# S5 parameters laid out by the host with the walked index contiguous, and the within-chunk products formed for four column groups at a time

## The chip, the cores and the metric

The kernel runs on one core of a Trainium2 chip. The metric is device time in microseconds for one execution, from inputs in device memory to the output in device memory. Rearranging inputs on the host (transposing or copying arrays before the launch) is not part of that time.

The engines named below are TensorE (PE in the profile; its weight loads are PEld), VectorE (DVE), ScalarE (ACT), GpSimd (POOL) and SyncE (SP). SyncE issues nearly all DMAs of this kernel, in one queue and in program order.

## The reference

The program is a two-layer residual trunk over 256 tokens of 2048 channels in float32. Layer 0 mixes tokens by stick-breaking attention and gated linear attention, layer 1 by a block-diagonal state-space model (S5); each layer then has a SwiGLU feed-forward part. The part that matters here is S5. 128 groups of 16 channels have 64 complex states each:

```python
lb_re, lb_im = mag * jnp.cos(ang), mag * jnp.sin(ang)            # lambda, per group and state
bb_re = cr[..., None] * b_re - ci[..., None] * b_im              # B scaled; b: (group, p, h)
bu_re = jnp.einsum('blgh,gph->blgp', u, bb_re)
_, _, s_re, s_im = lax.associative_scan(combine, (a_re, a_im, bu_re, bu_im), axis=1)
y = (jnp.einsum('ghp,blgp->blgh', c_re, s_re)                    # c: (group, h, p)
     - jnp.einsum('ghp,blgp->blgh', c_im, s_im) + d_skip * u)
```

Here h is one of 16 channels of a group and p one of its 64 states. The kernel does not scan token by token: it takes 32 chunks of 8 tokens. For that it prepares, from the parameters alone, three sets of matrices per group: `win` (lambda^(7-j) B: from the tokens of a chunk into the state), `ed` (C lambda^m: from the state to the tokens) and `td` (the real part of C lambda^(j'-j) B, with D on its diagonal: from token to token inside a chunk).

## The kernel before, in words

**The linear layers.** All large products multiply the 256 tokens by streamed weights. A chunk of weights is 4 k-tiles by 512 columns, 1 MB, brought by one DMA on SP's queue (`wraw`, line 100, three buffers). Each chunk is split in two units of 2 k-tiles: ScalarE writes the high part (`whi`), VectorE the low part (`wlo`), five buffers each, and a unit is split three units before it is used. TensorE then runs 12 matmuls of 512 columns per unit (lines 190 to 192, high by high, high by low, low by high, for two token blocks). TensorE executes in program order.

**Background work.** After each unit the program calls `pump`. It advances a list of generators, each up to its next `yield`, as long as an estimate of VectorE and ScalarE time stays within a budget. `s5_prep` is such a generator. It has nothing to do with the layer being computed (the feed-forward part of layer 0) and only has to be through before layer 1 begins. One `yield` is thus one unit of the linear layer further on, 12 large matmuls. The instructions between two yields stand in each engine's queue at that place.

**What s5_prep does, in order.** It forms lambda and its powers (`lam`, 9 powers side by side, so one power of successive states lies 36 bytes apart). It scales B by a factor per state and the norm gain. ScalarE spreads B into `bb` and a DMA writes it to the array `bb_d` in device memory. Then 32 steps multiply C by powers of lambda: four multiplies, one subtraction and one combined operation of 128 x 288 elements on VectorE per step, into `ed` and `tt`, and a DMA to `e_d` (lines 1142 to 1157).

Then come the products within a chunk: 16 iterations k of two halves. For a half, four DMAs (`fetch`, line 1170) bring pieces of `e_d` and `bb_d` into one of two buffers in the tile `et`; TensorE multiplies them (line 1213) into two of the four 32-row column groups of an accumulator; ScalarE copies 64 rows of it to `kp`, which also lies in the tile `et`, in one of two slots. After both halves VectorE adds D. After every second k, eight DMAs write `kp` to `t_d` (line 1222). A half's pieces are fetched one half ahead (`nxt`). One k takes seven yields.

The generator `win` runs beside the products: 28 steps of four multiplies and two sums of 128 x 256 elements, and four copies by lambda to the power zero in two parts, each followed by a DMA to `win_d` (line 1194).

When the products, `win` and the input product of the feed-forward part are done, the loads of the first `win` matrices from device memory into the tiles `ring` are issued (line 1240); the remaining loads for S5 (`w`, `t`, the second filling of `ring`, `eb`: lines 1240, 1244, 1249) follow when layer 1 begins.

Of the kernel before, what the change touches and what calls it, by code (L numbers as in the profile page):

```python
"""One core: residual trunk (stick-breaking + GLA mixer, S5 mixer, SwiGLU) in Tile.

Every weight product runs as three float32r passes on exactly split operands:
w = wh + wl, x = xh + xl (each part 12 significant bits), xh.wh + xh.wl + xl.wh.
"""
# [46 lines left out]
class Eng:  # L52
    """An engine's builders; adds up an estimate of the time of what they emit."""
# [23 lines left out]
class Stream:  # L77
    """Weights: 4 k-tiles x 512 columns per DMA, split by 2 k-tiles, ahead of their use."""
# [45 lines left out]
    def fill_extra(self):  # L124
        """one unit more, into a buffer that another part of the program has left"""
        if self.extra and len(self.split) // 2 < len(self.loaded):
            self.convert(self.extra.pop(0))
            return 1
        return 0

    def reload(self):
        """the buffers of chunks that have been split are loaded anew, up to chunk `limit`, and lent from there on"""
        end = len(self.plan) if self.limit is None else self.limit
        while True:
            room = len(self.split) // 2 + self.raw_bufs
            if len(self.loaded) < min(end, room):
                self.load()
            elif self.loans and len(self.loaded) == end and end + self.lent < room:
                self.loans.pop(0)()
                self.lent += 1  # L140
            else:
                break

    def next(self, ahead):
        """the next unit; `ahead` units from it on are split when it returns"""
        self.fill(self.used + ahead)
        got, self.split[self.used] = self.split[self.used], None
        self.used += 1
        return got


class Kern:
# [5 lines left out]
    # ---- background work: generators advanced between the units of a linear layer.  # L158
    # They yield where another engine has to take over, or True where none has to.
# [34 lines left out]
    # ---- linear layer: out[tok, n] for 512-column blocks  # L194
    def linear(self, blocks, acts, evac, opening=None, mid=None, hooks=None, spare=None):
        """blocks: ids; acts: (hi, lo) per k-tile, each an AP [128, 256].
        opening(mm): emits the first units of the first block, returns how many.
        mid: token-block-major order over the last four units, mid() emitted within them;
        the second token block's evacuation is then left in self.tail.
        hooks: {unit of the first block: callable emitted ahead of it (unit + 0.5: after it)}  # L200
        spare(): buffers for units split ahead of the last block's end"""
# [50 lines left out]
    def pairwise(self, blocks, acts, evac, hooks):  # L252
        """two blocks side by side, chunk by chunk; hooks: {unit: callable emitted ahead of it}"""
# [24 lines left out]
    # ---- small pieces  # L278
    def rstds(self, sums, width=D, between=None):
        """1 / sqrt(sum(ss) / width + eps) of several [128, 4] partial sums of squares, step by step side by side"""  # L280
# [21 lines left out]
    def split_to(self, hi, lo, src, scale=None):  # L302
        """hi + lo = src * scale (scale: None or [128, 1]); src may be in PSUM"""
# [15 lines left out]
    def turn(self, tb, k4, gcol):  # L319
        """four k-tiles of h (token-major) -> acts, feature-major, times the norm gain, split"""  # L320
# [21 lines left out]
    def post(self, layer, which, final=False, hold=()):  # L342
        """the evacuation of a sub-layer's output: y -> h += rms_norm(y) * gain.
        returns evac(nb, tb, ps) and the part that closes a token block"""
# [45 lines left out]
    # ---- plan of the weight stream  # L390
# [32 lines left out]
    # ---- SwiGLU  # L423
    def ffn(self, layer, final, mid, enter):
        """enter(): closes the pools of the mixer, when the first units have been emitted"""
# [140 lines left out]
    # ---- layer 0: stick-breaking attention and GLA  # L566
# [89 lines left out]
    def feat(self, src, dst):  # L656
        """[128 tok, 2, 512] -> [128, 4, 256] feature-major"""
# [9 lines left out]
    def softplus_neg_abs(self, dst, src):  # L667
        """dst = log(1 + exp(-|src|))"""
        nc = self.nc
        nc.scalar.activation(dst, src, AF.Abs)  # L670
        nc.scalar.activation(dst, dst, AF.Exp, scale=-1.0)
        nc.scalar.activation(dst, dst, AF.Ln, bias=1.0)

    def gla_gate(self, n0, tb, ps, rs):
        """sr = silu(r) * gain, r = ps * rs"""
# [12 lines left out]
    def gla(self, rs):  # L688
# [3 lines left out]
        # low-rank gate  # L692
# [61 lines left out]
        # scores, transposed: S[s, head, t] (even heads, then odd ones) for the token-tile pairs (0,0), (0,1), (1,1)  # L754
# [23 lines left out]
        for li, b in enumerate((64, 32, 16, 8, 4, 2, 1)):  # L778
            yield from self.need(2 * b + 1)
            mix = self.got.pop(2 * b + 1)  # L780
            # only the later halves of the blocks of 2 b tokens take part as t; even and odd heads at once
# [16 lines left out]
        # outputs  # L798
# [43 lines left out]
    def gla_levels(self):  # L842
        """k exp(cum_mid - cum_s) in the first halves, q exp(cum_t - cum_mid) in the second ones, per block size"""
# [40 lines left out]
    def sb_group(self, g):  # L884
        """four stick-breaking heads"""
# [55 lines left out]
    # ---- layer 1: S5, 32 chunks of 8 tokens. Token t = 8 c + j; group 8 k + 2 q + e holds the  # L941
    # channels 128 k + 32 q + 16 e + h; its state p is at partition (e, p), column 4 k + q.
    def s5_prep(self):
        """chunk matrices of the state space, from its parameters (partition = group (e, 4 k + q)), to DRAM:
        win[(h, j), (ri, p)] = lam^(7-j) B, ed[p, (m, h')] = C lam^m, td[(h, j), (j', h')] = Re C lam^(j'-j) B (+ D)"""
# [50 lines left out]
        # sine and cosine of th  # L996
# [50 lines left out]
        # (lam - 1) / lambda  # L1047
# [16 lines left out]
        # lam^8 at (e, p), column 4 k + q  # L1064
# [32 lines left out]
        # B, times the norm gain  # L1097
        B = st("B").rearrange("g (r p h) -> g r p h", r=2, p=64)
# [4 lines left out]
        for p0 in range(0, 64, 16):  # L1103
            ps = slice(p0, p0 + 16)
            n = pw([128, 2, 16, 16], "bt")
            crb, cib = (c[:, ps].unsqueeze(2).to_broadcast([128, 16, 16]) for c in (cr, ci))
            gb = g16.unsqueeze(1).to_broadcast([128, 16, 16])
            V.tensor_mul(n[:, 0], cib, B[:, 1, ps])
            V.tensor_mul(n[:, 1], cib, B[:, 0, ps])
            V.tensor_mul(B[:, 0, ps], crb, B[:, 0, ps])  # L1110
            yield True
            V.tensor_mul(B[:, 1, ps], crb, B[:, 1, ps])
            V.tensor_sub(B[:, 0, ps], B[:, 0, ps], n[:, 0])
            V.tensor_add(B[:, 1, ps], B[:, 1, ps], n[:, 1])
            yield True
            V.tensor_mul(B[:, 0, ps], B[:, 0, ps], gb)
            V.tensor_mul(B[:, 1, ps], B[:, 1, ps], gb)
# [9 lines left out]
        for p0 in range(0, 64, 8):  # L1127
            flush()
            o = pw([128, 2, 8, 2, 16], "bb")
            for ri in range(2):  # L1130
                for e in range(2):
                    nc.scalar.activation(o[:, ri, :, e, :], B[:, ri, p0:p0 + 8], AF.Identity, scale=self.sel[:, e:e + 1])
            late.append(lambda o=o, p0=p0: dma(bb_g[:, :, p0:p0 + 8], o.rearrange("g r p e h -> g r p (e h)")))
            yield
        # C
        flush()
        C = st("C").rearrange("g (r h p) -> g r h p", r=2, h=16)
# [4 lines left out]
        for p0 in range(0, 64, 2):  # L1142
# [3 lines left out]
            c = [C[:, ri, :, p0:p0 + 2].rearrange("g h p -> g p h").unsqueeze(2).to_broadcast([128, 2, 9, 16]) for ri in range(2)]  # L1146
# [13 lines left out]
        # the products within a chunk  # L1160
# [12 lines left out]
        def win():  # L1173
            late = []
            for h0 in range(0, 16, 4):
                b = [B[:, ri, :, h0:h0 + 4].rearrange("g p h -> g h p") for ri in range(2)]
# [24 lines left out]
        nxt = fetch(0)  # L1201
        for k in range(16):
            for half in range(2):
                et, bt = nxt
                if 2 * k + half < 31:
                    nxt = fetch(2 * k + half + 1)
                yield
                yield
                p = self.pbig([128, 128])
                for ri in range(2):  # L1210
                    for q in range(2):
                        r = 64 * half + 32 * q
                        nc.tensor.matmul(p[r:r + 32, :], lhsT=bt[:, q, ri, :], rhs=et[:, q, ri, 0:128], start=(ri == 0), stop=(ri == 1))  # L1213
                yield
                pr = slice(64 * half, 64 * half + 64)
                nc.scalar.copy(kp[pr, k % 2, 112:240], p[pr])
# [17 lines left out]
    def s5_load(self, what, u, t):  # L1234
        """matrices of the groups of the channel tiles 2 u and 2 u + 1 ("t1", "e": of the channel tile u; "e" with zero between even and odd groups)"""
# [16 lines left out]
    def layer1(self):  # L1252
# [3 lines left out]
        def normed(tb, nb, r, eng):  # L1256
            """normalized h, without the gain, over the sub-layer's output"""
# [41 lines left out]
        def scan(hf):  # L1299
            """by pairs of chunks: within them, along the even chunks, from those to the odd ones;  # L1300
            yields where an operation waits for the one before it, four times in a step"""
# [143 lines left out]
        def out(G, n=0):  # L1445
            """channel tiles 4 G to 4 G + 3"""
# [81 lines left out]
def host_layout(inputs):  # L1528
    """the inputs as they are; the parameters of S5 with the even groups ahead of the odd ones"""
    arrays = {n: np.ascontiguousarray(inputs[n]) for n in INPUTS}  # L1530
    for n in INPUTS:
        if n.startswith("s5_") and n != "s5_d":
            a = arrays[n][0]
            arrays[n] = np.ascontiguousarray(a.reshape((64, 2) + a.shape[1:]).swapaxes(0, 1).reshape((1,) + a.shape))
# [16 lines left out]
```

## Time and profile before

| what | value |
|---|---|
| median of 3 runs | 2232.69 us (2229.08 to 2235.0) |
| span of the profiled execution | 2230.8 us (its time outside the span is not listed) |
| TensorE busy | 2175.5 us (98%) |
| VectorE busy | 1376.8 us (62%) |
| ScalarE busy | 985.1 us (44%) |
| DMA traffic | 456.36 MB, mean 205 GB/s |
| products within a chunk (line 1213) | 832.1 to 1176.9 us of the span, 256 matmuls |

In the profile, PE, PEld, DVE, ACT, POOL and SP are the engines, and "L1213" is line 1213 of the kernel. Most VectorE and ScalarE operations are recorded through one helper, line 65, so they are told apart by the tiles they write and read: `wlo<-wraw,whi` is the low part of a weight unit. A group row gives total busy time and the mean of one in nanoseconds, and behind the bar the idle time just before, with what ended it. In a timeline row the first number is the start in us from the span's beginning, the second the length of the merged run. TensorE's matmuls overlap: a large one is listed with 0.39 us though they start 0.23 us apart.

### The profile page before, as it was taken

What the parts mean: (1) busy time and instruction counts of PE and PEld (TensorE: products, weight loads), DVE (VectorE), ACT (ScalarE), POOL (GpSimd) and SP (SyncE); (2) the same over time, 40 slices, a digit from 0 to 9 for tenths busy, and PEclk for the clock granted to TensorE, in tenths of its full rate; (3) what the DMA queues carried; (4) which work ended last, traced back from release to release, by engine and by line L of the source; (5) the groups of instructions that cost most, each with busy time, mean ns of one, the idle gap of its engine ahead of it and who ended that gap; (6) DMA issues with size and microseconds to landing.
All of it is one profiled execution on the core that took longest, in us unless ns stands there. A gap on an engine that the chain in (4) does not pass through costs nothing.

```text
span 2230.8 us, 26592 instructions
## 1 busy us (share of the span) xinstructions
PE 2175.5 (98%) x10448; PEld 1751.4 (79%) x10448; DVE 1376.8 (62%) x1917; ACT 985.1 (44%) x1242; POOL 16.0 (1%) x19
## 2 busy tenths in 40 slices
PE   8999999999999999999998699999999999999998
PEld 6888888788888887777776578878888888888886
DVE  4676645658779997895456765475444444444545
ACT  5544545454544444334344434464444434433433
POOL 0000000000000000000000100000000000000000
PEclk9999999999999999999999999999999999999999
DMA  7454454554677678998779976546555545555543
GB/s 227 169 179 157 164 170 152 188 209 170 223 241 250 226 249 241 276 281 263 225 229 271 274 223 201 176 171 214 181 189 171 206 171 195 181 190 188 188 171 133
DMA packets 318653, 456.36 MB, mean 205 GB/s; under 512 B 31136, under 2 KB 127664, under 8 KB 318016
## 3 DMA queue, kind: packets, MB, share of 16 engines
q1 hardware_dynamic: 317808, 449.95, 62.3%
q0 software_dynamic: 720, 4.72, 0.6%
q8 instruction: 82, 1.34, 0.2%
q14 instruction: 43, 0.35, 0.0%
HBM read 424.21 MB, written 30.41 MB: 204 GB/s over the span
## 4 chain that ended last, share of the span: by engine, by line
PE 91%; DVE 3%; DMA 2%; ACT 1%; issue 1%; SPq 1%; POOL 0%; DVEq 0%; ACTq 0%; POOLq 0%
PE lin L190 28%; PE lin L192 28%; PE lin L191 28%; PE big L465 1%; DMA eb<-e_d 1%; DVE wlo L65 1%; PE big L1213 1%; PE big L192 0%; PE big L792 0%; PE big L191 0%; PE big L190 0%; DVE h L65 0%; DVE xl L65 0%; ACT xh L65 0%; DMA ring<-e_d 0%
## 5 line engine op out<-in xcount | busy, mean ns | idle before, releaser
L65 DVE TENSOR_TENSOR wlo<-wraw,whi 128x1024 fp32r<-128x1024 f32 x713 | 860.3, 1223 | 562.1 <-ACT whi L65 561.6
L65 ACT CAST whi<-wraw 128x1024 fp32r<-128x1024 f32 x713 | 731.3, 1049 | 650.3 <-PE lin L192 575.1
L190 PE MATMUL lin<-whi,xh 128*128 128x512 f32 x2016 | 803.1, 398 | 3.5 <-ACT xh L65 3.5
L191 PE MATMUL lin<-wlo,xh 128*128 128x512 f32 x2016 | 796.9, 395 | 2.3 <-DVE wlo L65 2.1
L192 PE MATMUL lin<-whi,xl 128*128 128x512 f32 x2016 | 796.6, 395 | 0.9 <-DVE xl L65 0.9
L190 PEld LDWEIGHTS lin<-whi,xh 128*128 128x128 f32 x2016 | 380.2, 189 | 95.2 <-issue 5.0
L191 PEld LDWEIGHTS lin<-wlo,xh 128*128 128x128 f32 x2016 | 380.2, 189 | 91.2 <-DVE wlo L65 5.7
L192 PEld LDWEIGHTS lin<-whi,xl 128*128 128x128 f32 x2016 | 380.0, 188 | 90.9 <-DVE xl L65 2.5
L190 PE MATMUL lin<-whi,ah 128*128 128x512 f32 x680 | 270.2, 397 | 0.0
L192 PE MATMUL lin<-whi,al 128*128 128x512 f32 x680 | 268.4, 395 | 0.0
L191 PE MATMUL lin<-wlo,ah 128*128 128x512 f32 x680 | 268.3, 395 | 0.0
L190 PEld LDWEIGHTS lin<-whi,ah 128*128 128x128 f32 x680 | 127.7, 188 | 32.3 <-issue 2.6
L192 PEld LDWEIGHTS lin<-whi,al 128*128 128x128 f32 x680 | 127.7, 188 | 30.8
L191 PEld LDWEIGHTS lin<-wlo,ah 128*128 128x128 f32 x680 | 127.7, 188 | 30.0
L65 DVE SCALAR_TENSOR_TENSOR a<-lin,rs,a 128x512 f32<-128x512 f32 x44 | 31.0, 746 | 60.0 <-PE lin L192 60.0
L65 ACT ACTIVATE a<-lin,rs 128x512 f32<-128x512 f32 x44 | 27.9, 685 | 90.7 <-PE lin L192 90.7
L65 ACT ACTIVATE junk<-yg 128x512 f32<-128x512 f32 x24 | 15.2, 632 | 74.7 <-DVE yg L65 74.7
L65 ACT CAST ah<-big 128x1024 fp32r<-128x1024 f32 x22 | 22.3, 1016 | 55.4 <-PE big L465 55.4
L65 DVE TENSOR_TENSOR ed<-C,lam 128x288 f32<-128x288 f32 x64 | 43.4, 678 | 5.0 <-DMA wraw<-w_ffn_out 5.0
L65 DVE TENSOR_TENSOR yg<-lin,yg 128x512 f32<-128x512 f32 x30 | 19.9, 688 | 41.0 <-PE lin L192 41.0
L65 DVE TENSOR_TENSOR tt<-lam,B 128x256 f32<-128x256 f32 x56 | 36.7, 656 | 11.0 <-DMA win_d<-win 11.0
L65 DVE TENSOR_TENSOR tt<-C,lam 128x288 f32<-128x288 f32 x64 | 43.3, 677 | 0.3 <-DMA C<-s_c_im 0.3
(300 smaller groups left out, 1284.4 us busy)
## 6 DMA issues: line engine op xcount, KB each, us to landing
wraw<-w_ffn_in SPq DMA_DIRECT2D x176, 1024.0 KB, 4.9
wraw<-w_ffn_out SPq DMA_DIRECT2D x88, 1024.0 KB, 5.5
wraw<-w_in SPq DMA_DIRECT2D x47, 1024.0 KB, 5.0
wraw<-w_glu SPq DMA_DIRECT2D x32, 1024.0 KB, 6.1
wraw<-w_out SPq DMA_DIRECT2D x16, 1024.0 KB, 5.1
e_d<-ed SPq DMA_DIRECT2D x32, 288.0 KB, 5.0
et<-e_d SPq DMA_DIRECT2D x64, 144.0 KB, 5.5
win_d<-win SPq DMA_DIRECT2D x32, 256.0 KB, 5.9
```

The costliest lines, as they stand in the source:

```text
L65: return f(*a, **k)
L190: mm(ps, lhsT=xh, rhs=hi[:, kk, :], start=(k == 0), stop=False)
L191: mm(ps, lhsT=xh, rhs=lo[:, kk, :], start=False, stop=False)
L192: mm(ps, lhsT=xl, rhs=hi[:, kk, :], start=False, stop=(k == len(acts) - 1))
L465: nc.tensor.transpose(p[:, tb, i, :], a[:, tb, i * 128:(i + 1) * 128], self.ident)
L1213: nc.tensor.matmul(p[r:r + 32, :], lhsT=bt[:, q, ri, :], rhs=et[:, q, ri, 0:128], start=(ri == 0), stop=(ri == 1))
```

## The change

The host now stores the three-dimensional S5 parameters with their last two indices exchanged: B as (h, p), C as (p, h). Three parts of `s5_prep` follow:

- B is scaled in four steps of 4 channels by 64 states instead of 16 states by 16 channels; the number and size of the operations stay. The `bb` copies on ScalarE now read B with a stride of 256 bytes, where they read it in sequence before. The multiplies of `win` read B in sequence, where the stride was 64 bytes; their other operand, a power of lambda, keeps its stride.
- The multiplies by C read C in sequence, where the stride was 256 bytes.
- The products within a chunk run per k: both halves are fetched at the head of the iteration (eight DMAs), three yields later 16 TensorE instructions (eight float32 matmuls, each of them two) go to four column groups, one ScalarE copy takes all 128 rows after a further yield, then D is added, another yield, and after every second k the eight writes to `t_d`. One k takes five yields. Nothing is fetched ahead of its own iteration.

Comments and docstrings are also taken out, so that a few line numbers move: 1213 becomes 1210, 1222 becomes 1218, 1240 becomes 1236, 1244 becomes 1240, 1249 becomes 1245.

```diff
-        B = st("B").rearrange("g (r p h) -> g r p h", r=2, p=64)
+        B = st("B").rearrange("g (r h p) -> g r h p", r=2, h=16)
...
-        for p0 in range(0, 64, 16):
-            ps = slice(p0, p0 + 16)
-            n = pw([128, 2, 16, 16], "bt")
-            crb, cib = (c[:, ps].unsqueeze(2).to_broadcast([128, 16, 16]) for c in (cr, ci))
-            gb = g16.unsqueeze(1).to_broadcast([128, 16, 16])
+        for h0 in range(0, 16, 4):
+            hs = slice(h0, h0 + 4)
+            n = pw([128, 2, 4, 64], "bt")
+            crb, cib = (c.unsqueeze(1).to_broadcast([128, 4, 64]) for c in (cr, ci))
+            gb = g16[:, hs].unsqueeze(2).to_broadcast([128, 4, 64])
...
-                    nc.scalar.activation(o[:, ri, :, e, :], B[:, ri, p0:p0 + 8], AF.Identity, scale=self.sel[:, e:e + 1])
+                    nc.scalar.activation(o[:, ri, :, e, :], B[:, ri, :, p0:p0 + 8].rearrange("g h p -> g p h"), AF.Identity, scale=self.sel[:, e:e + 1])
...
-        C = st("C").rearrange("g (r h p) -> g r h p", r=2, h=16)
+        C = st("C").rearrange("g (r p h) -> g r p h", r=2, p=64)
...
-            c = [C[:, ri, :, p0:p0 + 2].rearrange("g h p -> g p h").unsqueeze(2).to_broadcast([128, 2, 9, 16]) for ri in range(2)]
+            c = [C[:, ri, p0:p0 + 2].unsqueeze(2).to_broadcast([128, 2, 9, 16]) for ri in range(2)]
...
-                b = [B[:, ri, :, h0:h0 + 4].rearrange("g p h -> g h p") for ri in range(2)]
+                b = [B[:, ri, h0:h0 + 4] for ri in range(2)]
...
-        nxt = fetch(0)
         for k in range(16):
-            for half in range(2):
-                et, bt = nxt
-                if 2 * k + half < 31:
-                    nxt = fetch(2 * k + half + 1)
-                yield
-                yield
-                p = self.pbig([128, 128])
-                for ri in range(2):
-                    for q in range(2):
-                        r = 64 * half + 32 * q
-                        nc.tensor.matmul(p[r:r + 32, :], lhsT=bt[:, q, ri, :], rhs=et[:, q, ri, 0:128], start=(ri == 0), stop=(ri == 1))
-                yield
-                pr = slice(64 * half, 64 * half + 64)
-                nc.scalar.copy(kp[pr, k % 2, 112:240], p[pr])
+            parts = [fetch(2 * k + half) for half in range(2)]
+            yield
+            yield
+            yield
+            p = self.pbig([128, 128])
+            for ri in range(2):
+                for n in range(4):
+                    et, bt = parts[n // 2]
+                    nc.tensor.matmul(p[32 * n:32 * n + 32, :], lhsT=bt[:, n % 2, ri, :], rhs=et[:, n % 2, ri, 0:128], start=(ri == 0), stop=(ri == 1))
+            yield
+            nc.scalar.copy(kp[:, k % 2, 112:240], p)
             V.scalar_tensor_tensor(kp[:, k % 2, 112:128], self.sel[:, 2:18], dp[:, k:k + 1], kp[:, k % 2, 112:128], op0=mul, op1=add)
             yield
             if k % 2:
...
+            if a.ndim == 3:
+                a = a.swapaxes(1, 2)
```

How the change moves instructions, at three places. First TensorE, at the products of k = 0 inside the first linear layer that they meet (`lin_6158` is that layer's accumulator, `xh` and `xl` its activations, `big` the product's accumulator; x4 and x8 count matmuls of one shape, each of which appears twice in the profile). One half's product goes:

```order
 L191 MATMUL lin_6158<-wlo_6160,xh_91 128x512
 L192 MATMUL lin_6158<-whi_6159,xl_92 128x512
-L1213 MATMUL big_6245<-et_6177 32x128 x4
 L190 MATMUL lin_6158<-whi_6187,xh_91 128x512
 L191 MATMUL lin_6158<-wlo_6188,xh_91 128x512
```

and one unit (12 large matmuls) later the product for all four column groups comes:

```order
 L191 MATMUL lin_6158<-wlo_6188,xh_91 128x512
 L192 MATMUL lin_6158<-whi_6187,xl_92 128x512
+L1210 MATMUL big_6269<-et_6177 32x128 x8
 L190 MATMUL lin_6158<-whi_6208,xh_91 128x512
 L191 MATMUL lin_6158<-wlo_6209,xh_91 128x512
```

Over the whole run there are 32 products of x4 before, and 16 of x8 now. From one to the next stand 60 large matmuls (12 times) or 72 (three times: behind k = 0, 3 and 13); before it was 36 and 48 in turn from half to half, with 60 in place of 48 five times.

Second, SP's queue at the first writes to `t_d`, behind k = 1. Before:

```order
L1194 DMA win_d<-win_6481 128x4x128
L100 DMA wraw_6563<-w_ffn_out 128x4x512
L1222 DMA t_d<-et_6177 128x2x128 x8
L1170 DMA et_6177<-e_d 64x4x144 x2
L1170 DMA et_6177<-bb_d 64x4x32 x2
L1194 DMA win_d<-win_6529 128x4x128
L1194 DMA win_d<-win_6590 128x4x128
L100 DMA wraw_6619<-w_ffn_out 128x4x512
```

Now:

```order
L1194 DMA win_d<-win_6353 128x4x128
L100 DMA wraw_6465<-w_ffn_in 128x4x512
L1218 DMA t_d<-et_6177 128x2x128 x8
L1170 DMA et_6177<-e_d 64x4x144 x2
L1170 DMA et_6177<-bb_d 64x4x32 x2
L1170 DMA et_6177<-e_d 64x4x144 x2
L1170 DMA et_6177<-bb_d 64x4x32 x2
L1194 DMA win_d<-win_6435 128x4x128
L100 DMA wraw_6524<-w_ffn_in 128x4x512
```

Behind the eight writes stand eight fetches in place of four, and they bring what the very next product reads. Before, the four were for the second product behind them; the pieces of the first had been fetched ahead of the writes.

Third, SP's queue at the end of the layer. Before:

```order
L100 DMA wraw_8906<-w_ffn_out 128x4x512
L100 DMA wraw_8947<-w_ffn_out 128x4x512
L1222 DMA t_d<-et_6177 128x2x128 x8
L1240 DMA ring_8969<-win_d 128x8x128 x2
L1240 DMA ring_8970<-win_d 128x8x128 x2
L1240 DMA ring_8971<-win_d 128x8x128 x4
L1240 DMA w_9000<-win_d 128x8x128 x2
```

Now:

```order
L100 DMA wraw_8656<-w_ffn_out 128x4x512
L1236 DMA ring_8679<-win_d 128x8x128 x2
L1236 DMA ring_8680<-win_d 128x8x128 x2
L1236 DMA ring_8681<-win_d 128x8x128 x4
L100 DMA wraw_8712<-w_ffn_out 128x4x512
L100 DMA wraw_8746<-w_ffn_out 128x4x512
```

The last writes to `t_d` now stand ten weight chunks ahead of the loads of `ring`, and seven weight chunks (`wraw_8712` is the first) follow those loads before the `w` tiles.

More of the change, by code (lines that the diff above doesn't have):

```diff
@@ L1102, in s5_prep @@
         yield
-        for p0 in range(0, 64, 16):
-            ps = slice(p0, p0 + 16)
-            n = pw([128, 2, 16, 16], "bt")
-            crb, cib = (c[:, ps].unsqueeze(2).to_broadcast([128, 16, 16]) for c in (cr, ci))
-            gb = g16.unsqueeze(1).to_broadcast([128, 16, 16])
-            V.tensor_mul(n[:, 0], cib, B[:, 1, ps])
-            V.tensor_mul(n[:, 1], cib, B[:, 0, ps])
-            V.tensor_mul(B[:, 0, ps], crb, B[:, 0, ps])
+        for h0 in range(0, 16, 4):
[3 more added lines that the diff above has]
+            gb = g16[:, hs].unsqueeze(2).to_broadcast([128, 4, 64])
+            V.tensor_mul(n[:, 0], cib, B[:, 1, hs])
+            V.tensor_mul(n[:, 1], cib, B[:, 0, hs])
+            V.tensor_mul(B[:, 0, hs], crb, B[:, 0, hs])
             yield True
-            V.tensor_mul(B[:, 1, ps], crb, B[:, 1, ps])
-            V.tensor_sub(B[:, 0, ps], B[:, 0, ps], n[:, 0])
-            V.tensor_add(B[:, 1, ps], B[:, 1, ps], n[:, 1])
+            V.tensor_mul(B[:, 1, hs], crb, B[:, 1, hs])
+            V.tensor_sub(B[:, 0, hs], B[:, 0, hs], n[:, 0])
+            V.tensor_add(B[:, 1, hs], B[:, 1, hs], n[:, 1])
             yield True
-            V.tensor_mul(B[:, 0, ps], B[:, 0, ps], gb)
-            V.tensor_mul(B[:, 1, ps], B[:, 1, ps], gb)
+            V.tensor_mul(B[:, 0, hs], B[:, 0, hs], gb)
+            V.tensor_mul(B[:, 1, hs], B[:, 1, hs], gb)
             yield True
```

## The prediction

> **What bounds the kernel now.** I read the page's totals and the shares of its chain first, then the stages in which the changed code runs.
>
> ```profile
> span 2230.8 us, 26592 instructions
> PE 2175.5 (98%) x10448; PEld 1751.4 (79%) x10448; DVE 1376.8 (62%) x1917; ACT 985.1 (44%) x1242; POOL 16.0 (1%) x19
> PE 91%; DVE 3%; DMA 2%; ACT 1%; issue 1%; SPq 1%; POOL 0%; DVEq 0%; ACTq 0%; POOLq 0%
> ```
>
> TensorE is busy for 98% of the span and is 91% of the chain that ended last. The averages hide where the other engines come close, so I cut the span into the stretches of the changed code (columns: width, then busy time and number for PE, PEld, DVE, ACT, POOL; clock, DMA share, GB/s).
>
> ```profile
> 680.00:740.00 60.00, 60.00 (x260) 48.65 (x259) 57.99 (x89) 25.30 (x28) 0.00 (x0) 1.00 0.72 244
> 860.00:920.00 60.00, 59.62 (x283) 46.21 (x283) 49.83 (x77) 25.89 (x32) 0.00 (x0) 1.00 0.89 261
> 920.00:980.00 60.00, 60.00 (x287) 46.32 (x286) 52.13 (x81) 22.22 (x28) 0.00 (x0) 1.00 0.94 276
> ```
>
> In 680 to 740 the products of C with the powers of lambda fill VectorE: 57.99 of 60 us. TensorE beside it is busy for all 60. From 860 on, where the products within a chunk run (832 to 1177), the 16 DMA engines are at 0.89 to 0.94. From 540 to 1180 the list of TensorE's waits has one line:
>
> ```profile
> PE big L465 <- DVE a L65: 0.4, 1, 0.4
> ```
>
> So VectorE or ScalarE time saved there gives nothing by itself; what counts is what TensorE has to execute itself, and whether a wait appears that is not there now.
>
> **The products on TensorE.** One half of a product (L1213) among the matmuls of the linear layer:
>
> ```profile
> 899.84 0.39 PE L190 MATMUL lin<-whi,ah 128*128 128x512 f32 x1
> ...
> 902.86 0.39 PE L191 MATMUL lin<-wlo,ah 128*128 128x512 f32 x1
> 903.09 0.40 PE L192 MATMUL lin<-whi,al 128*128 128x512 f32 x1
> 903.42 0.63 PE L1213 MATMUL big<-et 128*32 128x128 f32 x8
> 903.98 0.50 PE L190 MATMUL lin<-whi,ah 128*128 128x512 f32 x1
> 904.31 0.39 PE L191 MATMUL lin<-wlo,ah 128*128 128x512 f32 x1
> L1213 PE MATMUL big<-et x256: 272/273/297, 832.1 to 1176.9; 128*32 128x128 f32 x128
> ```
>
> From 899.84 to 902.86 there are 13 steps, 0.232 us each. From 903.09 to 904.31 are two such steps (0.46) and the half: 1.22 - 0.46 = 0.76 us. Its eight matmuls of 0.273 end 0.63 after the first starts, so their starts lie (0.63 - 0.27) / 7 = 0.051 us apart: 0.41 for eight, and 0.35 for the change to the small tile and back. The 32 halves cost 32 x 0.76 = 24.3 us. After the change there are 16 visits with 16 matmuls each, on four column groups in turn. That form stands elsewhere in this kernel, in S5 itself (chain of waits; start, length):
>
> ```profile
> 1244.32 3.81 PE lin L1389 x128
> ```
>
> That is 3.81 / 128 = 0.030 us each. A visit then costs 0.35 + 16 x 0.030 = 0.83 us, 16 visits 13.2: **11.0 us less**. If four groups ran no closer than two do, a visit would be 0.35 + 16 x 0.051 = 1.17, together 18.7: 5.6 less. I take 11.0, since L1389 has the same contraction of 128 rows, 32 output rows and 128 columns.
>
> [...]
>
> **VectorE and ScalarE.**
>
> ```profile
> L65 DVE TENSOR_TENSOR ed<-C,lam 128x288 f32<-128x288 f32 x64 | 43.4, 678 | 5.0 <-DMA wraw<-w_ffn_out 5.0
> L65 DVE TENSOR_TENSOR ed<-ed,tt 128x288 f32<-128x288 f32 x32 | 14.6, 457 | 0.0
> L65 DVE TENSOR_TENSOR win<-lam,B 128x256 f32<-128x256 f32 x56 | 36.8, 657 | 0.0
> L65 DVE TENSOR_TENSOR win<-win,tt 128x256 f32<-128x256 f32 x56 | 21.3, 427 | 0.0
> L65 DVE TENSOR_TENSOR sm<-lam 128x64 f32<-128x64 f32 x14 | 3.9, 278 | 0.0
> L65 DVE TENSOR_TENSOR sm<-sm 128x64 f32<-128x64 f32 x20 | 4.0, 222 | 0.4
> ```
>
> The multiplies by C read it 256 bytes apart now and in sequence after: 678 - 457 = 221 ns off each of 128 (64 into ed and 64 into tt), 28 us of VectorE. At TensorE that is worth 0: in the stretch where it falls TensorE doesn't wait. If the cover were gone, it would be at most 28. The multiplies for win lose B's stride of 64 bytes, but lambda's powers are still read 36 bytes apart, and a strided lambda alone costs (278 - 222) / 64 = 0.9 ns an element, 224 for 256 elements: 427 + 224 = 651, what is measured now with both operands strided. So I take nothing; the other end is 230 ns off each of 112, 26 us of VectorE, hidden as well. [...]
>
> ScalarE loses 16 copies from the accumulator and reads B strided for the bb rows, which are 32 operations in all. Neither can exceed a few us spread over hundreds on an engine that is 44% busy; TensorE gets 0 from it. The multiplies that scale B keep their number and size: 0.
>
> **The fetches: a wait that may appear.** Now the pieces for a half are fetched a half ahead. After the change both halves are fetched at the head of their own iteration, behind the eight t_d writes where there are any, into the buffers that the product before has just read. All stand in SP's queue in order (start, length):
>
> ```profile
> 874.26 6.21 SPq L1222 DMA_DIRECT2D t_d<-et  x8
> 880.60 1.24 SPq L1170 DMA_DIRECT2D et<-e_d  x2
> 881.88 1.27 SPq L1170 DMA_DIRECT2D et<-bb_d  x2
> ...
> 916.05 8.59 SPq L1222 DMA_DIRECT2D t_d<-et  x8
> ...
> 960.09 6.36 SPq L1222 DMA_DIRECT2D t_d<-et  x8
> ...
> 1132.03 4.50 SPq L1222 DMA_DIRECT2D t_d<-et  x8
> et<-bb_d SPq DMA_DIRECT2D x2, 32.0 KB, 2.5
> et<-bb_d SPq DMA_DIRECT2D x61, 32.0 KB, 4.7
> ```
>
> The last two rows are landing times, 2.5 us for the two issued between 880.5 and 883.2, right behind the writes, and a median of 4.7 over 830 to 1180. The products whose copies those writes send (chain of waits), and the product that read the fetch at 880.60 (timeline):
>
> ```profile
> 866.04 0.56 PE big L1213 x8
> 912.64 0.56 PE big L1213 x8
> 954.88 0.56 PE big L1213 x8
> 1130.86 0.56 PE big L1213 x8
> 887.01 0.63 PE L1213 MATMUL big<-et 128*32 128x128 f32 x8
> ```
>
> From 866.04 to 887.01 are 21 us, seven units of the linear layer. The chain inside: 8.2 until the first write is issued (copy and correction wait in line behind a block's evacuation), 6.3 for eight writes, then four fetches; the last is issued near 882.5 and lands 2.5 later, at 885.0. So 2.0 us are to spare in the worst of these places.
>
> After the change the order puts five units between the same two products, 60 large matmuls: 60 x 0.232 + 0.83 = 14.8 us; at two of the seven places behind writes it is 72 (17.6, and eight transposes more). The chain is D + 6.3 (eight writes) + 7 x 0.635 (fetches ahead of the last, half of 1.27 each) + 2.5 = D + 13.2, with D from product to first write. So TensorE waits for D - 1.6 where 60 stand, and not where 72 do unless D exceeds 4.4. D in the rows is 8.2, 3.4, 5.2 and 1.2. The first includes an evacuation; the mean of the other three is 3.3. That makes 1.7 at each of five places: **8.5 us more**. Behind the even products there are no writes: D + 7 x 0.635 + 4.7 (the median landing) stays under 14.8 up to D = 5.7: 0. Bounds: with D as low as 1.2 nothing; with 5.2 at all five, 18.
>
> What queues behind: weight loads and win_d writes stand on SP behind the 16 instead of 12 DMAs, 2.5 us later. Three raw chunks and three split units of lead cover that, unless the DMA engines, at 0.94, fall behind; that is in the second rival.
>
> **The entry to S5.** The products end some 100 us earlier, and the loads of win into the ring move from behind the last weight chunk to seven chunks ahead of it.
>
> ```profile
> 1189.77 10.96 SPq L1240 DMA_DIRECT2D ring<-win_d  x8
> ...
> 1225.62 15.01 SPq L1244 DMA_DIRECT2D ring<-t_d  x4
> 1240.73 4.04 SPq L100 DMA_DIRECT2D wraw<-w_glu  x3
> 1237.58 3.63 PE lin L1369 x64
> PE big L1389 <- issue: 1.6, 1, 1.6
> PE big L1369 <- issue: 1.3, 1, 1.3
> ```
>
> The later loads wait for TensorE to leave the ring and the raw buffers (L1369 in the chain runs until 1241.2), so the 11 us saved on the queue are mostly not on the path. The two gaps of 1.6 and 1.3 that the profile gives no releaser for stand where ring and w tiles are read; I take half of them, **1.5 less**. Bounds: 3 less; 5 more, if the 11 us burst now makes weight chunks late by a part of its own length.
>
> **Sum.** 2230.8 - 11.0 + 8.5 - 1.5 = 2226.8 of span. The median of the runs lies 1.9 above the profiled span (2232.7 against 2230.8; the execution's time outside its span isn't listed): 2228.7, call it **2229**, with 2224 to 2234 for this case alone. About 0.3%, 6.7 us, is what a measurement of this kernel can tell from no change: faster is below 2226.0, slower above 2239.4.
>
> **Rivals.** *The fetches are always in time.* For it: D was 1.2 at 1130.86, where no win multiplies stood ahead of the correction, and all transfers are shorter where the queue is quiet. Against: until the win part is through, D is 3.4 and more. Time: 2230.8 - 11.0 - 1.5 + 1.9 = 2220.
>
> *The fetches are late and the lateness feeds itself (slower).* The place is each burst of 16 DMAs behind an odd product. With D at 5.2 and a landing of 4.7 instead of 2.5, TensorE waits 5.2 - 1.6 + 2.2 = 5.8 at five places, 29 together; with the short landing 18. That gives 2238 to 2249, middle 2244. It decides from 3.8 us a burst on (19.2 together makes 2239.4). For it: fetches and writes that lay in 345 us now lie in some 240, with DMA already at 0.94, and only 2.0 us were to spare at seven units. Against: while TensorE waits, VectorE works off what makes D long, and landing right behind a burst was short.
>
> *Four column groups gain no overlap.* Saving 5.6 in place of 11.0, with the same waits: 2234. The 0.030 of L1389 speaks against it. That the change doesn't do what it says is excluded by the order: products of 16 matmuls in place of 8, half as many.
>
> **Chances.** Forecast 0.45 (0.11 of it under 2226.0), in time 0.27, late 0.20, no overlap 0.08. Faster 0.11 + 0.27 = 0.38; slower 0.19 of the late case and 0.01 of the last, 0.20; same 0.42. The range goes from 2217 (the full gain with the 3 us at the entry is 2218) to 2243, which leaves out half of the late case.
>
> **What would show it.** The products as 16 matmuls of 0.7 to 0.8 us between large ones (right), or over 1.1 (third rival). A line "PE big" at the products, waiting for a fetch, with about 8 us: right; none: first rival; 20 or more: second. VectorE's ed rows near 457 ns and win rows near 650. It is wrong altogether if TensorE's busy time falls by much less than 11 us, or if waits for weights appear between 830 and 1100.

## The result, and the profile after

The changed kernel takes 2245.5 us (median of 4 runs, 2242.8 to 2246.4) against 2232.2 before (2229.1 to 2235.0): a ratio of 1.0054, 95% interval 1.0039 to 1.0068. It is slower by 0.5%, and outside the predicted range of 2217 to 2243. The page of the changed kernel:

```profile
span 2243.0 us, 26582 instructions
PE 2179.5 (97%) x10448; PEld 1757.4 (78%) x10448; DVE 1350.1 (60%) x1917; ACT 982.5 (44%) x1226; POOL 16.0 (1%) x19
PE 88%; DVE 5%; DMA 4%; SPq 2%; ACT 1%; issue 1%; POOL 0%; DVEq 0%; ACTq 0%; POOLq 0%
```

VectorE has 27 us less to do, and TensorE's share of the chain fell from 91% to 88%: more of VectorE, of DMAs and of SP's queue stands in it now. TensorE's busy time did not fall by the 11 us of the prediction, it rose by 4.0; slow matmuls, listed with 0.63 us where others have 0.39, add to it. TensorE's waits from 540 to 1190, where there was one of 0.4 us, are now this line, and the stretch of the products looks as follows (width, then busy time and number for PE, PEld, DVE, ACT, POOL; clock, DMA share, GB/s):

```profile
PE big L1210 <- DMA et<-bb_d: 15.5, 10, 2.5
830.00:1130.00 300.00, 284.31 (x1398) 222.89 (x1397) 203.19 (x290) 107.32 (x125) 0.00 (x0) 0.97 0.88 258
830.00:880.00 50.00, 45.68 (x232) 35.70 (x231) 39.42 (x61) 18.00 (x23) 0.00 (x0) 0.97 0.89 258
930.00:980.00 50.00, 43.15 (x205) 33.09 (x204) 34.69 (x56) 14.76 (x18) 0.00 (x0) 0.91 0.90 254
980.00:1030.00 50.00, 49.15 (x245) 38.34 (x245) 41.66 (x66) 16.86 (x20) 0.00 (x0) 0.99 0.98 295
1030.00:1080.00 50.00, 46.33 (x233) 36.18 (x232) 22.40 (x22) 19.13 (x22) 0.00 (x0) 0.97 0.86 253
```

Two things are new. TensorE stands still for 15.5 us in ten pieces, waiting for the fetched parts of B and C. And the granted clock, 1.00 in all these stretches before, is 0.91 to 0.99 in four of them. The shares by which it lies under 1.00 add up to (0.03 + 0.09 + 0.01 + 0.03) x 50 = 8.0 us lost, an estimate from the clock of these four rows. What this is in single instructions is seen at the first of the waits, behind the first writes to `t_d`. TensorE's timeline, with the product of k = 1 and, in two pieces, that of k = 2:

```profile
851.98 0.40 PE L192 MATMUL lin<-whi,xl 128*128 128x512 f32 x1
852.30 0.65 PE L1210 MATMUL big<-et 128*32 128x128 f32 x16
852.88 0.50 PE L190 MATMUL lin<-whi,xh 128*128 128x512 f32 x1
853.22 0.39 PE L191 MATMUL lin<-wlo,xh 128*128 128x512 f32 x1
...
869.33 0.41 PE L1210 MATMUL big<-et 128*32 128x128 f32 x4 [2.18 <-DMA et<-bb_d]
871.88 1.07 PE L1210 MATMUL big<-et 128*32 128x128 f32 x12 [2.13 <-DMA et<-bb_d]
872.87 0.80 PE L190 MATMUL lin<-whi,xh 128*128 128x512 f32 x1
873.47 0.63 PE L191 MATMUL lin<-wlo,xh 128*128 128x512 f32 x1
873.89 0.63 PE L192 MATMUL lin<-whi,xl 128*128 128x512 f32 x1
```

and SP's queue between the two products:

```profile
857.70 6.53 SPq L1218 DMA_DIRECT2D t_d<-et  x8
864.36 1.65 SPq L1170 DMA_DIRECT2D et<-e_d  x2
866.19 1.23 SPq L1170 DMA_DIRECT2D et<-bb_d  x2
867.52 1.23 SPq L1170 DMA_DIRECT2D et<-e_d  x2
868.79 1.28 SPq L1170 DMA_DIRECT2D et<-bb_d  x2
```

The chain is the one of the prediction: 5.4 us from the product at 852.30 to the first write, 6.7 for the writes, 5.1 until the last fetch is issued (868.79 + 0.64), 2.4 until it has landed and the second part of the product starts at 871.88. TensorE had been done with the units between since about 867 and waits 2.18 for the first half's pieces and 2.13 for the second's. Then the large matmuls start 0.42 to 0.60 us apart instead of 0.23; from 875.45 on it is 0.23 again. At this place the waits are followed by matmuls at about half speed.

VectorE's rows came out as expected: 451 ns for the multiplies by C where it was 678, and no change worth naming for `win`.

```profile
L65 DVE TENSOR_TENSOR ed<-C,lam 128x288 f32<-128x288 f32 x64 | 28.8, 451 | 6.0 <-DMA wraw<-w_ffn_out 6.0
L65 DVE TENSOR_TENSOR win<-lam,B 128x256 f32<-128x256 f32 x56 | 36.3, 648 | 0.0
```

### The profile page after: what moved, and what is told of

Its sections match the earlier page's. It is cut to its first block, busy times and chain, and to the rows that moved or that the text cites. A ratio compares the mean times of both kernels' runs of the same rounds, so it can differ in the third digit from the quotient of the medians.

```text
span 2243.0 us, 26582 instructions
## 1 busy us (share of the span) xinstructions
PE 2179.5 (97%) x10448; PEld 1757.4 (78%) x10448; DVE 1350.1 (60%) x1917; ACT 982.5 (44%) x1226; POOL 16.0 (1%) x19
## 4 chain that ended last, share of the span: by engine, by line
PE 88%; DVE 5%; DMA 4%; SPq 2%; ACT 1%; issue 1%; POOL 0%; DVEq 0%; ACTq 0%; POOLq 0%
PE lin L190 27%; PE lin L191 27%; PE lin L192 27%; DMA t_d<-et 1%; DVE wlo L65 1%; SPq L1170 1%; PE big L465 1%; DMA eb<-e_d 1%; DMA et<-bb_d 1%; DVE win L65 1%; PE big L192 0%; PE big L792 0%; PE big L191 0%; PE big L190 0%; DVE h L65 0%
## 5 line engine op out<-in xcount | busy, mean ns | idle before, releaser
L65 DVE TENSOR_TENSOR al<-big,ah 128x1024 fp32r<-128x1024 f32 x22 | 26.9, 1223 | 16.3 <-ACT ah L65 16.2
L65 DVE TENSOR_TENSOR win<-lam,B 128x256 f32<-128x256 f32 x56 | 36.3, 648 | 0.0
```

The source lines that it names most:

```text
L65: return f(*a, **k)
```

## The experiments

The theory to be tested is called the fetch theory: the 12 us that the span grew are 15.5 us of waits and some 8 us lost to a halved clock, less the saving of the products. Rivals: the layout costs the time; the products for four column groups cost it; the DMA engines are simply full.

**One part of the change at a time.** First the layout alone, with the old loop over halves:

```diff
-            parts = [fetch(2 * k + half) for half in range(2)]
-            ... (the loop of the change)
+        nxt = fetch(0)
+            ... (the loop of the kernel before)
```

> Only the host layout of B and C and the code that reads them; the products within a chunk are as before (32 halves, fetched a half ahead). Fetch theory (the loss comes from TensorE waiting for the fetches and from the half clock behind those waits; the layout is worth nothing to TensorE): 2231, 2228 to 2235, no wait for a fetch, VectorE's multiplies by C near 451 ns as in the changed kernel. Layout rival (the strided reads of B on ScalarE or the other order of B cost the 13 us): 2240 to 2246.

Measured: 2234.0, ratio 1.0005 (0.9996 to 1.0013). TensorE's only wait from 540 to 1190 is again the 0.4 us of before; VectorE's multiplies by C take 452 ns. The layout is worth nothing to TensorE in either direction, though it takes 28 us from VectorE. Then the new loop alone, with the old layout (the same diff the other way round, on the kernel before):

> Only the products within a chunk in the new form, with the old host layout. Fetch theory: as slow as the changed kernel or a little slower, since VectorE is busier and the correction of D is reached later: 2242 to 2252, waits for fetches of 13 to 22 us and stretches of half clock. Layout rival: 2217 to 2224, the saving of the products alone.

Measured: 2244.1, ratio 1.0046 (1.0033 to 1.0060), 16.0 us of waits for fetches. The whole loss lies in the new loop.

**The order in the queue.** The next k's fetches are issued right behind the product, ahead of the copy, the correction and the writes:

```diff
+        parts = [fetch(half) for half in range(2)]
         for k in range(16):
-            parts = [fetch(2 * k + half) for half in range(2)]
...
                     nc.tensor.matmul(p[32 * n:32 * n + 32, :], ...)
+            if k < 15:
+                parts = [fetch(2 * k + 2 + half) for half in range(2)]
             yield
             nc.scalar.copy(kp[:, k % 2, 112:240], p)
```

> The changed kernel, with the eight fetches of the next k issued right behind the product of k, ahead of the copy, the correction of D and the writes to t_d. Nothing else differs and no buffer is added. Fetch theory: the chain behind a product is only eight issues (5 us) and a landing (2.5 to 5), which 14.8 us hold: no wait for a fetch, full clock through 830 to 1180, and the saving of the products stays: 2232.2 - 11.8 = 2220, 2216 to 2224. If the waits come from DMA engines at 0.98 and not from the order in the queue, some 8 us of waits stay and the time is 2228 to 2236. If the products for four column groups slow TensorE by themselves, it stays above 2236.

Measured: 2219.5 (2216.7 to 2221.4), ratio 0.9939 (0.9926 to 0.9952). Waits and stretch of this kernel, to be read against those of the changed one:

```profile
PE big L1210 <- DMA et<-bb_d: 0.8, 2, 0.5
830.00:1130.00 300.00, 299.20 (x1502) 236.53 (x1501) 214.54 (x301) 118.17 (x137) 0.00 (x0) 1.00 0.93 272
```

The loss became a gain by the place of the fetches in the order alone. The DMA engines are busier than in the changed kernel, 0.93 against 0.88, and the same products run: neither full engines nor the four column groups were the cause. SP's queue behind the product of k = 2 shows what was gained (the first of four rows, two fetches each):

```profile
868.15 1.47 SPq L1170 DMA_DIRECT2D et<-e_d  x2
```

That product starts at 867.48, and the fetches for k = 3 start 0.7 us later. Of the clock, nothing is lost from 830 to 1130.

**The price of the half clock.** Where TensorE waited longest, it was given useless large matmuls to do. Nothing is left out of the computation; work is added (`self.last` holds the operands of the linear layer's latest matmul).

```diff
+            warm = {2: 14, 6: 9, 8: 12, 14: 7}.get(k, 0)
+            if warm:
+                p = self.pbig([128, 512])
+                for _ in range(warm):
+                    nc.tensor.matmul(p, lhsT=self.last[0], rhs=self.last[1], start=True, stop=True)
             p = self.pbig([128, 128])
```

> The changed kernel with useless large matmuls ahead of the products of k = 2, 6, 8 and 14, where TensorE waited 4.3, 2.9, 4.0 and 2.3 us: 14, 9, 12 and 7 of them, 0.23 us each, 9.8 us of work together, so that it works in place of most of the wait. Their results are not read. Fetch theory with the half clock behind waits: the waits are filled and not lengthened, the clock stays at full speed in 830 to 1180, and the some 17 us at half clock (8.5 us lost) go: 2237, 2234 to 2240. If the lowered clock has another cause than the idle time, or costs nothing: 2244 or more.

Measured: 2240.7 (2237.2 to 2244.1), ratio 1.0035 (1.0023 to 1.0047); the span is 4.1 us shorter than the changed kernel's. That is just outside the expected 2234 to 2240. Four of its stretches:

```profile
830.00:880.00 50.00, 48.63 (x251) 38.24 (x250) 36.94 (x57) 18.01 (x23) 0.00 (x0) 1.00 0.87 256
880.00:930.00 50.00, 47.45 (x239) 36.99 (x238) 42.14 (x65) 18.68 (x22) 0.00 (x0) 0.97 0.88 252
930.00:980.00 50.00, 47.91 (x242) 37.31 (x241) 38.00 (x61) 15.81 (x19) 0.00 (x0) 1.00 0.94 269
1030.00:1080.00 50.00, 48.00 (x246) 37.60 (x245) 22.40 (x22) 18.98 (x22) 0.00 (x0) 1.00 0.85 250
```

The clock is 1.00 wherever the waits were filled. It is 0.97 only in 880 to 930, where a wait of 2.5 us appeared at k = 4, which had none. So between these two runs the lowered clock went with the waits: in the same stretches 830 to 880, 930 to 980 and 1030 to 1080 the changed kernel had 0.97, 0.91 and 0.97. What it is worth in time is shown less well. The sum of waits and added work is 9.8 + 9.4 = 19.2 us against 15.5, 3.7 more; the clock's loss fell from 8.0 to some 1.5 by the same estimate, which leaves 2.8 of gain. Over the stretch of the products, from a large matmul ahead of the first of them to the last large one of the layer, 1.8 were measured; the rest of the 4.1 arose later, in S5, where this edit changes nothing. And the intervals of the two ratios, 1.0023 to 1.0047 here and 1.0039 to 1.0068 for the change, overlap. So added work of 9.8 us cost nothing, and that it made the kernel faster is likely, not shown.

**What in the chain counts.** Only the writes and the fetches exchanged, both left at the place in the loop where the fetches are:

```diff
             parts = [fetch(2 * k + half) for half in range(2)]
+            if k and k % 2 == 0:
+                put(k - 1)          # the eight writes to t_d
             yield
...
-            if k % 2:
-                (the eight writes to t_d)
+        put(15)                     # behind the loop
```

> The changed kernel with two blocks exchanged in the queue: the eight writes to t_d of a pair of k stand behind the eight fetches of the next k instead of ahead of them. The fetches stay at the head of their own iteration, two yields later than in the run that fetches right behind the product. Chain theory (TensorE waits because the fetches stand behind the correction of D and 6.3 us of writes): without them the chain is the place in the queue, 5 us of issues and a landing of 2.5 to 5, under 14.8: waits under 2, no half clock, 2218 to 2224. If the look-ahead by itself is too short (three yields, 8.4 us, between fetch and product), 5 us or more of waits stay: 2228 or more.

Measured: 2230.2, ratio 0.9996 (0.9987 to 1.0006): as fast as the kernel before, some 13 us better than the change by the ratios, and not the full gain. The waits:

```profile
PE big L1217 <- DMA et<-bb_d: 5.8, 8, 1.3
```

Ahead of the even k, where the writes had stood, nothing is left. The waits are now ahead of odd k, where there were none. One of them, on SP's queue and then TensorE, behind the product of k = 4 at 901.61:

```profile
907.02 1.49 SPq L1170 DMA_DIRECT2D et<-e_d  x2
...
912.03 4.82 SPq L1170 DMA_DIRECT2D et<-bb_d  x2
...
917.73 0.41 PE L1217 MATMUL big<-et 128*32 128x128 f32 x4 [1.33 <-DMA et<-bb_d]
918.62 0.63 PE L1217 MATMUL big<-et 128*32 128x128 f32 x12 [0.48 <-DMA et<-bb_d]
```

The fetches begin 5.4 us after the product, because they stand two units and their weight loads further down the queue. The issue of the last pair takes 4.8 us instead of 1.3; why, no view shows. Behind these two waits, 1.8 us together, the large matmuls start 0.43 us apart for 3.4 us. So the second alternative of the expectation holds: with the eight fetches in their own iteration the look-ahead itself is too short, by a little. By the ratios, half of the way from 1.0054 to 0.9939 comes from the order of writes and fetches (to 0.9996), the other half from fetching two units earlier.

Then the order of the change, with four fetches of twice the size:

```diff
-            c = 704 * (n % 2)
-            et, bt = ... for a, b in ((c, c + 576), (c + 576, c + 704))
+            et, bt = ... for a, b in ((0, 1152), (1152, 1408))
...
-                    dma(d[64 * e:64 * e + 64], s[e, 2 * n:2 * n + 2]....)
+                    dma(d[64 * e:64 * e + 64], s[e, 4 * k:4 * k + 4]....)
```

> The changed kernel, its order unchanged, with four fetches per k of twice the size instead of eight. Chain theory: four issues of 0.63 us less in the chain, 2.5 us; with the D measured in the changed kernel (5.4, 4.8, 4.2, 2.9, 1.9, and 8.4 where 72 matmuls stand) the waits fall from 15.5 to 3 or 4, single ones stay under 2 us, and nothing runs at half clock: 2245.5 - 12 - 8.5 = 2225, 2221 to 2229. If it is the bytes and not the issues that take the time: waits of 10 or more and 2238 or more.

Measured: 2239.9, ratio 1.0037 (1.0024 to 1.0050), 14.9 us of waits. The chain theory was wrong on this number. The same place as above, SP's queue and TensorE, and the landing times in 864 to 872, here and (last row) in the changed kernel:

```profile
864.18 2.22 SPq L1169 DMA_DIRECT2D et<-e_d  x2
866.45 1.31 SPq L1169 DMA_DIRECT2D et<-bb_d  x2
870.86 1.08 PE L1209 MATMUL big<-et 128*32 128x128 f32 x16 [3.19 <-DMA et<-bb_d]
et<-bb_d SPq DMA_DIRECT2D x2, 64.0 KB, 3.8
et<-bb_d SPq DMA_DIRECT2D x4, 32.0 KB, 2.3
```

The last issue is 2.3 us earlier (867.8 against 870.1), but it lands later after its issue, 3.8 instead of 2.3. The product can start 1.0 us earlier, 870.86 against 871.88. And since the first part no longer starts ahead of the second, one wait of 3.2 takes the place of two of 2.2 and 2.1. So halving the number of DMAs for the 704 KB that a product needs saves little, as in the second alternative of the expectation. Whether the longer landing comes from the size of the pieces or from what else was under way (1.84 MB moved from 864 to 872, against 1.51) is not shown.

**Variants of the fast version.** The early fetches, and four of twice the size:

> Both: fetched right behind the product, and four DMAs of twice the size. No wait was left to take away but 0.8 us, so the same as the run that only fetches right behind the product, 2219.5: 2216 to 2222. If the queue of weight loads gains from eight issues fewer, up to 2 us less.

Measured: 2219.6, ratio 0.9948 (0.9935 to 0.9961), no wait for a fetch at all, and no faster. The early fetches with the loads of the ring held back, to price the entry to S5 (33 more yields ahead of `self.need("in", "win")`):

> The run that fetches right behind the product, with the loads of win into the ring held back until behind the last weight chunk of the layer, where they stood in the kernel before. This prices the entry to S5, put down as 1.5 us gained by the earlier loads (bounds: 3 gained, 5 lost): 2221 against 2219.5, 2219 to 2223. If the earlier burst costs the weight stream more than it gains: 2215 to 2219.

Measured: 2218.3, ratio 0.9939 (0.9924 to 0.9953), equal to the 0.9939 without this edit. Last, the early fetches with the old layout:

> The old host layout, with the products for four column groups and the fetches right behind the product: the run that gained 14 us, without the layout. If the layout is worth nothing to TensorE also when the fetches come early, 2219, 2217 to 2222, with VectorE 26 us busier. If the relief of VectorE is what lets the early fetches work (the writes, the copies and the weight splits come later with a busy VectorE): waits return, 2224 to 2232.

Measured: 2218.3, ratio 0.9938 (0.9925 to 0.9952), with VectorE's multiplies by C back at 675 ns. The layout adds nothing here either. The versions with early fetches lie within each other's intervals, 12 to 14 us under the kernel before and some 26 under the changed one.

## Why the prediction was wrong, point by point

- **What bounds the kernel:** right. VectorE lost 27 us and TensorE gained nothing (layout alone: 1.0005).
- **The products on TensorE:** right. From 851.98 to 853.22 are 1.24 us, less two steps of 0.232: 0.78 for a visit where 0.83 was put down. That is 24.3 - 16 x 0.78 = 11.8 us saved, against 11.0. The 5.6, the saving if four groups ran no closer than two do, is not borne out.
- **VectorE's rows:** right, 451 ns with C in sequence, and 648 for `win`, whose lambda is still read with a stride.
- **The place and the form of the waits:** right. There is a wait ahead of each even k from 2 to 14 but for k = 4, and none ahead of odd k. The constant of the chain was put at 13.2 us behind D (in this list the time from a product to the first write; the S5 parameter D is called the parameter). At k = 2 it measured 19.6 - 5.4 = 14.2, with writes of 6.5 instead of 6.3 and slower issues, at k = 8 it is 975.1 - 960.2 = 15.0, with writes of 7.8.
- **The size of the waits:** too small, 8.5 against 15.5. The mean D of 3.3 was taken from three rows; at the five places with 60 matmuls it measured 5.4, 4.8, 4.2, 2.9 and 1.9, a mean of 3.8. And a place with 72 was taken as free unless D exceeds 4.4; there, behind k = 13, D was 8.4. The profile before had eight such places, and the four that the prediction left out have a D of 4.3, 8.3, 6.7 and 5.9. The mean of all eight is 5.4, and by the prediction's own formula that would have been 5.4 - 1.6 = 3.8 us at each of five places, 19 together. The row of 8.2 had been set aside because an evacuation stood in it. What made D long behind k = 13 was something else, a weight load ahead of the writes (VectorE, then SP, then the product that waited):

```profile
1061.63 1.22 DVE L65 TENSOR_TENSOR wlo<-wraw,whi 128x1024 fp32r<-128x1024 f32 x1
...
1062.87 0.37 SPq L100 DMA_DIRECT2D wraw<-w_ffn_in  x1
1063.29 5.73 SPq L1218 DMA_DIRECT2D t_d<-et  x8
...
1074.17 0.41 PE L1210 MATMUL big<-et 128*32 128x128 f32 x4 [0.82 <-DMA et<-bb_d]
1076.04 0.63 PE L1210 MATMUL big<-et 128*32 128x128 f32 x12 [1.46 <-DMA et<-bb_d]
```

The product of k = 13 starts at 1054.91 and the parameter is added by 1057.7. The writes could go then, but a weight load stands ahead of them in the queue and is issued when the split that ends at 1062.85 has left its buffer. At k = 1 it is the same: the parameter added by 854.9, the weight load at 857.28, the writes at 857.70. The order of the change shows that weight load just ahead of the writes. The profile before shows it too, here behind the product at 1039.36, with the parameter added by 1042.1:

```profile
1033.45 14.18 SPq L100 DMA_DIRECT2D wraw<-w_ffn_in  x3
1047.68 5.28 SPq L1222 DMA_DIRECT2D t_d<-et  x8
```

The third of these weight loads is issued at 1047.26, just ahead of the writes. In the row of 8.2 the parameter is added by 871.4, and a weight load at 873.84 stands ahead of the writes at 874.26.
- **The step that failed:** the waits were priced at their own length. The sum had no term for what TensorE does behind a wait. Matmuls at half clock cost 8.0 us here by the estimate from the clock, nearly as much as the whole predicted wait. Either mistake alone, waits of 15.5 for 8.5 or no 8.0 for the clock, would have left the forecast at 2236 or 2237, inside its range; both together take it to 2244, outside. With the new term the sum comes near: -11.8 + 15.5 + 8.0 = 11.7, against 12.2 measured between the spans. It does not close fully: over the stretch of the products alone (a large matmul at 828.09 before and 827.07 now, the last one of the layer at 1207.63 and 1220.09) the change lost 13.5 us, so some 2 are unexplained there, and 1.3 came back elsewhere. The trace shows the halving at four places: behind the waits of k = 2, 6 and 14 the granted clock is 0.50 for 3.4 us, behind those of k = 8 for 6.8, with matmuls 0.43 us apart where it was 0.23.
- **The entry to S5:** 1.5 us of gain were put down and 0.3 measured (the spans differ by 12.2 at the end and by 12.5 at the layer's last large matmul); holding the loads back made no difference (0.9939 in both).
- **The rivals:** the slower one gave the right sign, with waits of 18 to 29 us; but the condition that it named, 3.8 us a burst, was not met (15.5 over six places is 2.6 each), so that its time came out is luck. The missing part was the clock and not self-feeding lateness: over the five places with 60 matmuls D fell from 5.4 to 1.9, as had been argued against that rival.

## What to carry to other kernels

A fetch that used to be issued one step ahead must keep its place in the queue when two steps are merged into one: ask what stands ahead of it there, and issue loads for the next product as soon as their buffer is free, ahead of writes that nobody waits for. Here eight loads, moved ahead of the writes and two units earlier, were worth 26 us. Read every row of a wait's chain that the profile has before you take a mean, and ask of each what stood ahead of it in the queue. Waits of TensorE are to be priced with the slow matmuls that a trace shows behind them, which here, by the estimate from the clock, made them half as expensive again (8.0 on 15.5). An engine's busy time in a stretch, here VectorE's 97% from 680 to 740 before, is no reason to relieve it as long as TensorE doesn't wait for it there (layout alone: 1.0005).

## What the runs showed of the hardware that was not expected

Waits of a few us were followed by a lowered clock, but not all of them. In the changed kernel:

| k | waits ahead of the product, us | behind them |
|---|---|---|
| 2 | 2.18 and 2.13 | clock 0.50 for 3.4 us |
| 6 | 1.08 and 1.80 | clock 0.50 for 3.4 us |
| 8 | 1.53 and 2.45 | clock 0.50 for 6.8 us |
| 10 | 0.70 | clock 1.00, large matmuls 0.23 us apart |
| 12 | 1.39 | clock 1.00, large matmuls 0.23 us apart |
| 14 | 0.82 and 1.46 | clock 0.50 for 3.4 us |

The rows below are the places at k = 2 and k = 14, each first with the 3.41 us in which its waits lie for the most part and then with the slow stretch (width, then PE busy time first; clock third from last):

```profile
868.40:871.81 3.41, 0.41 (x4) 0.17 (x4) 1.23 (x1) 0.98 (x2) 0.00 (x0) 1.00 0.64 151
871.81:875.23 3.42, 3.35 (x18) 2.52 (x19) 0.64 (x2) 1.82 (x4) 0.00 (x0) 0.50 0.95 255
1073.20:1076.61 3.41, 1.13 (x18) 0.55 (x17) 0.00 (x0) 0.00 (x0) 0.00 (x0) 1.00 0.67 129
1076.61:1080.02 3.41, 3.41 (x10) 2.73 (x9) 1.46 (x2) 1.21 (x2) 0.00 (x0) 0.50 1.04 399
```

By the profile's listing TensorE is idle for 3.00 us of the first row and for 2.28 of the third. In the run with larger fetches the large matmuls behind the waits of 3.19 and 3.26 us start 0.43 us apart, but behind those of 1.84 and 2.15 they keep their 0.23. The place of the 2.15:

```profile
1072.47 0.64 PE L1209 MATMUL big<-et 128*32 128x128 f32 x16 [2.15 <-DMA et<-bb_d]
1073.04 0.50 PE L190 MATMUL lin<-whi,xh 128*128 128x512 f32 x1
1073.38 0.39 PE L191 MATMUL lin<-wlo,xh 128*128 128x512 f32 x1
1073.61 0.39 PE L192 MATMUL lin<-whi,xl 128*128 128x512 f32 x1
```

And in the run with writes and fetches exchanged, waits of 1.33 and 0.48 us, 1.8 together, were followed by 3.4 us of matmuls 0.43 us apart. So in these runs the length of the waits alone does not tell whether slow matmuls follow, 1.8 us in two pieces against 2.15 in one; what else decides was not shown.
